# One low part in four by an accumulating transfer in a split-float32 decoder layer

## The chip, the cores and the metric

The kernel runs on one core of one Trainium2 chip. The metric is the device time of one execution in microseconds (us). Beside it stands the span of a profiled execution, from the first to the last instruction that the profiler recorded on that core.

## The reference, cut to what matters

A decoder layer on x of 256 x 2048, float32. Everything hangs on large products with weights that are read once from memory:

```python
proj = jnp.einsum('btd,dc->btc', x, w_in[l])      # 2048 -> 17 thousand columns
(q_lat, c_kv, attn_gate, q_idx, k_idx, w_idx,
 x_rnn, rnn_gate, g_a, g_b) = jnp.split(proj, SPLIT_POINTS, axis=-1)
attn = _sparse_attention(q_lat, c_kv, q_idx, k_idx, w_idx, rel_bias, w_uv[l])
branch_a = jnp.einsum('btc,cd->btd', attn * jax.nn.silu(attn_gate), w_branch_a[l])
h = _rglru(x_rnn, ...)
branch_b = jnp.einsum('btc,cd->btd', h * jax.nn.silu(rnn_gate), w_branch_b[l])
merged = jax.nn.sigmoid(g_a) * branch_a + jax.nn.sigmoid(g_b) * branch_b
sub = jnp.einsum('btd,de->bte', merged, w_out[l])
x = _layernorm(ALPHA * x + sub, ln_g[l], ln_b[l])
```

## The kernel before, in words

Each float32 operand of a product is split in two values of the narrower type that TensorE multiplies (float32r): a high part `hi`, the operand rounded to it, and a low part `lo = operand - hi`. A product is then hi·hi + hi·lo + lo·hi.

**Half tiles.** The weights come as 328 half tiles of 128 x 1024 float32, 512 KB each, numbered in the order in which TensorE uses them. A job is a column tile of 128 columns (two halves: `qi`, `ag`, `q`, `xr`, `rg`) or a chunk of 512 columns (eight halves: `ga`, `ba`, `gb`, `bb`). The order of the jobs is qi, ag, q, ga, ba, xr, gb, rg, bb; the last 32 halves are the output projection, `o`. In a column tile the weights are the stationary operand: the first half runs 8 products with `hi` of 512 columns, then 8 with `lo` of 256; the second half runs `lo` first and `hi` last (L203). In a chunk the activations are stationary, and a half is 12 products of 512 columns in the order hi, lo, hi (L756, L757, L758).

**Rings.** `load_to` (L163) brings a half into one of 4 `raw` buffers by a transfer issued by SyncE. `split_to` (L178) makes `hi` (ScalarE, helper line L96) and `lo` (VectorE, helper line L100, a subtraction of `hi` from `raw`), each from a ring of 5 buffers. Both are called from the main loop: while TensorE works on half n, the program issues the split of half n+4 and the load of half n+8. So the split of half i waits until TensorE has finished half i-5, whose buffers it takes, and it is used four halves later.

**Order of the rest.** Each engine runs its instructions in the order in which the program issues them. All other work (gates, attention heads, the recurrence) is cut into steps that the main loop issues at counted ticks, between the products. GpSimd has little: additions of the bias and the mask (L444), clearing of three columns (`xp`, L657), 16 multiplications for the recurrence (`decay`, L703), and at the start of the second `bb` chunk four transfers of 1 MB for the end of the layer (`gb` and `y`, L784 to L787), then one multiplication of `gb` (L877). The four transfers write into memory that the recurrence used, so they wait for its last scan (L711).

Of the kernel before, what the change touches and what calls it, by code (L numbers as in the profile page):

```python
# [13 lines left out]
AF = mybir.ActivationFunctionType  # L14
OP = mybir.AluOpType
# [57 lines left out]
def layer(ctx, tc, ar, out):  # L73
    nc = tc.nc
# [17 lines left out]
    def f(ap):  # L92
        return ap.bitcast(F32)

    def hi_of(hi, src):
        nc.scalar.activation(hi, src, AF.Copy)  # L96

    def lo_of(lo, src, hi):

        nc.vector.tensor_sub(lo, src, f(hi))  # L100
# [7 lines left out]
    def slot(name, dt=F32R):  # L108
        return big.tile([P, 2 * T], dt, name=name, tag="slot", bufs=16)
# [44 lines left out]
    halves = []  # L154
# [7 lines left out]
    raws, parts = {}, {}  # L162
    st = {"load": 0, "split": 0}  # L163

    def load_to(n):
        while st["load"] < min(n, len(halves)):
            i = st["load"]
            kind, a, s = halves[i]
            raw = wpool.tile([P, 1024], F32, name=f"raw{i}", tag="raw", bufs=4)
            if kind == "wt":  # L170
                src = ar["wt"][a, :, s * 8:(s + 1) * 8, :].rearrange("p k c -> p (k c)")
            else:
                src = ar[kind][a, s].rearrange("p k c -> p (k c)")
            nc.sync.dma_start(raw, src)
            raws[i] = raw
            st["load"] += 1

    def split_to(n):  # L178
        while st["split"] < min(n, len(halves)):
            i = st["split"]  # L180
            load_to(i + 1)
            raw = raws.pop(i)
            if NO + 24 <= i < NO + 28:
                pieces = []
                for e in range(2):
                    hi, lo = slot(f"wh{i}_{e}"), slot(f"wl{i}_{e}")
                    c = raw[:, e * 512:(e + 1) * 512]
                    hi_of(hi, c)
                    lo_of(lo, c, hi)
                    pieces.append((hi, lo))  # L190
                parts[i] = pieces
            else:
                hi = wpool.tile([P, 1024], F32R, name=f"hi{i}", tag="hi", bufs=5)
                lo = wpool.tile([P, 1024], F32R, name=f"lo{i}", tag="lo", bufs=5)
                hi_of(hi, raw)
                lo_of(lo, raw, hi)
                parts[i] = (hi, lo)
            st["split"] += 1

# [20 lines left out]
    with pool("pha", side="right") as pha:  # L220
# [29 lines left out]
        for k in range(KT):  # L250
            if k + 1 < KT:
                sp[k + 1] = split_a(k + 1)
            if k + 4 < KT:
                load_a(k + 4)
            else:
                load_to(st["load"] + 1)
            if 8 <= k < 12:
                nc.sync.dma_start(*smalls[k - 8])
            hi, lo = sp.pop(k)
            fl = (k == 0, k == KT - 1)  # L260
            for t in range(2):
                o = psc[t][:, :A_Q]
                x_hi = xs[:, k, t * P:(t + 1) * P]
                x_lo = xs[:, k, T + t * P:T + (t + 1) * P]
                nc.tensor.matmul(o, x_hi, hi[:, :A_Q], start=fl[0], stop=False)
                nc.tensor.matmul(o, x_hi, lo[:, :A_Q], start=False, stop=False)
                nc.tensor.matmul(o, x_lo, hi[:, :A_Q], start=False, stop=fl[1])
            last = k == KT - 1
            for high in (False, True) if last else (True, False):
                for i in range(4):  # L270
                    w = (hi if high else lo)[:, A_Q + i * P:A_Q + (i + 1) * P]
                    mm(psq[i], w, xs[:, k, :], high, fl[0] and high, last and high)
            if k >= 12:
                split_to(k - 11)
# [486 lines left out]
    for kind, i in jobs:  # L761
# [3 lines left out]
        for qt in range(ticks((kind, i))):  # L765
# [25 lines left out]
            else:  # L791
                high = qt in (0, 3)
                w = parts[t // 2][0 if high else 1]
                for kk in range(8):
                    k = qt // 2 * 8 + kk
# [4 lines left out]
            if qt % 2 == 0:  # L800
                split_to(t // 2 + 5)
                load_to(t // 2 + 9)
# [59 lines left out]
    for ec in range(3):  # L862
        pss = [acc_tile(f"pso{ec}_0"), aux_tile(f"pso{ec}_1")]
        for pc in range(8):
            n = NO + ec * 8 + pc
            for i in range(2):
                for t in range(2):
                    products(pss[t], parts[n], i, 2 * pc + i, xs[:, 2 * pc + i, :], t)
                tick(t0)
                t0 += 1  # L870
                if i == 0:
                    split_to(n + 5 + max(0, n - NO - 15) // 2)
                    load_to(n + 9 + max(0, n - NO - 15) // 2)
            parts.pop(n)
        spawn(t0, out_post(ec, pss))
        if ec == 0:
            nc.gpsimd.tensor_scalar(gb[0], gb[0], -0.5, None, op0=OP.mult)  # L877
# [67 lines left out]
```

## Time and profile before

| what | us |
|---|---|
| median of 2 runs (1031.92 to 1036.3) | 1034.11 |
| the profiled execution's own time | 1032.58 |
| its span | 1030.7 |
| TensorE busy | 1014.5 |
| VectorE busy | 683.2 |
| ScalarE busy | 550.8 |
| GpSimd busy | 83.9 |

The granted clock of TensorE was 0.997 over the span. In the profile PE is TensorE (PEld its weight loads), DVE is VectorE, ACT is ScalarE, POOL is GpSimd, SP is SyncE; q0 is the queue of the transfers that GpSimd issues, q1 that of SyncE's. Matmuls overlap in the pipeline, so a matmul's 0.39 us is not its share of the time: in a chunk one starts every 0.227 us. A row of the timeline gives start, duration, engine, line, operation, output and inputs; what stands in brackets is the idle time before it and what ended it. A row of a group gives the busy time, the mean of one in ns and the idle time before. A row of the transfers gives size and the median time from issue to landing.

### The profile page before, as it was taken

The numbers are of one execution on the slowest core, as the hardware profiler recorded it, in microseconds if no ns is written. First come the engines' busy times: TensorE is split into PE (matmuls) and PEld (weight loads), VectorE is DVE, ScalarE is ACT, GpSimd is POOL, SyncE is SP. The second block draws the span as 40 slices with busy tenths as digits, with TensorE's granted clock in tenths as the row PEclk, the third lists the DMA queues.
The fourth block names the chain that finished last, engine by engine and source line by source line (L and its number), as shares of the span: only waits on it lengthen the run. The fifth ranks groups of instructions, "written<-read, shape, count | busy, mean of one in ns | idle before, by whom it ended". The sixth has DMA issues, their size and how long they took to land.

```text
span 1030.7 us, 14867 instructions
## 1 busy us (share of the span) xinstructions
PE 1014.5 (98%) x5464; PEld 880.0 (85%) x5464; DVE 683.2 (66%) x1150; ACT 550.8 (53%) x909; POOL 83.9 (8%) x117
## 2 busy tenths in 40 slices
PE   9999999999999999999999999999999999999995
PEld 8988888988999988888888888888888887888885
DVE  6678587677777676444555788855567876555666
ACT  6666365655555656444343555578655554444441
POOL 0004211101111100000000000000410002000002
PEclk9999999999999999999999999999999999999998
DMA  9845867756566655666666666556666668666552
GB/s 303 271 144 175 280 192 230 231 174 173 184 181 178 194 165 162 187 200 187 198 190 210 204 190 191 164 183 193 194 187 191 189 220 303 189 187 192 188 160 82
DMA packets 60713, 201.41 MB, mean 195 GB/s; under 512 B 6577, under 2 KB 13361, under 8 KB 60001
## 3 DMA queue, kind: packets, MB, share of 16 engines
q1 hardware_dynamic: 59456, 191.35, 60.2%
q0 software_dynamic: 752, 8.42, 2.1%
q8 instruction: 43, 0.70, 0.3%
q10 hardware_dynamic: 432, 0.70, 0.2%
q14 instruction: 30, 0.24, 0.1%
HBM read 198.31 MB, written 6.32 MB: 199 GB/s over the span
## 4 chain that ended last, share of the span: by engine, by line
PE 93%; DVE 2%; ACT 1%; DMA 1%; issue 1%; POOL 0%; ACTq 0%; DVEq 0%; POOLq 0%
PE ps_q L203 17%; PE ps_rg L203 9%; PE ps_xr L203 9%; PE ps_ag L203 6%; PE ps_ga L756 3%; PE ps_gb L758 3%; PE ps_ga L757 3%; PE ps_ga L758 3%; PE ps_ba L757 3%; PE ps_ba L756 3%; PE ps_gb L756 3%; PE ps_gb L757 3%; PE ps_ba L758 3%; PE psq L203 2%; PE ps_bb L756 2%; PE ps_qi L203 2%
## 5 line engine op out<-in xcount | busy, mean ns | idle before, releaser
L100 DVE TENSOR_TENSOR lo<-raw,hi 128x1024 fp32r<-128x1024 f32 x324 | 402.9, 1244 | 308.8 <-ACT hi L96 304.9
L96 ACT ACTIVATE hi<-raw 128x1024 fp32r<-128x1024 f32 x324 | 341.4, 1054 | 185.4 <-PE ps_ba L758 52.6
L203 PE MATMUL ps_q<-xs,hi 128*128 128x512 f32 x512 | 122.4, 391 | 0.0
L203 PEld LDWEIGHTS ps_q<-xs,hi 128*128 128x128 f32 x512 | 94.1, 188 | 18.3
L203 PE MATMUL ps_q<-xs,lo 128*128 128x256 f32 x512 | 71.2, 283 | 0.0
L203 PEld LDWEIGHTS ps_q<-xs,lo 128*128 128x128 f32 x512 | 66.3, 190 | 1.4
L203 PE MATMUL ps_ag<-xs,hi 128*128 128x512 f32 x256 | 61.5, 391 | 0.0
L203 PE MATMUL ps_rg<-xs,hi 128*128 128x512 f32 x256 | 61.2, 391 | 0.0
L203 PE MATMUL ps_xr<-xs,hi 128*128 128x512 f32 x256 | 61.2, 391 | 0.0
L203 PEld LDWEIGHTS ps_ag<-xs,hi 128*128 128x128 f32 x256 | 47.0, 188 | 9.9 <-issue 0.9
L203 PEld LDWEIGHTS ps_rg<-xs,hi 128*128 128x128 f32 x256 | 47.0, 188 | 9.1
L203 PEld LDWEIGHTS ps_xr<-xs,hi 128*128 128x128 f32 x256 | 47.0, 188 | 9.1
L756 PE MATMUL ps_bb<-hi,ub 128*128 128x512 f32 x128 | 50.4, 394 | 0.0
L756 PE MATMUL ps_ga<-hi,xs 128*128 128x512 f32 x128 | 50.0, 391 | 0.0
L758 PE MATMUL ps_ga<-hi,xs 128*128 128x512 f32 x128 | 49.9, 390 | 0.0
L758 PE MATMUL ps_gb<-hi,xs 128*128 128x512 f32 x128 | 49.9, 390 | 0.0
L758 PE MATMUL ps_bb<-hi,ub 128*128 128x512 f32 x128 | 49.9, 389 | 0.0
L757 PE MATMUL ps_gb<-lo,xs 128*128 128x512 f32 x128 | 49.8, 389 | 0.0
L757 PE MATMUL ps_ga<-lo,xs 128*128 128x512 f32 x128 | 49.8, 389 | 0.0
L757 PE MATMUL ps_bb<-lo,ub 128*128 128x512 f32 x128 | 49.8, 389 | 0.0
L756 PE MATMUL ps_ba<-hi,ua 128*128 128x512 f32 x128 | 49.8, 389 | 0.0
L757 PE MATMUL ps_ba<-lo,ua 128*128 128x512 f32 x128 | 49.8, 389 | 0.0
(274 smaller groups left out, 1888.7 us busy)
## 6 DMA issues: line engine op xcount, KB each, us to landing
raw<-in_wt SPq DMA_DIRECT2D x168, 512.0 KB, 4.2
raw<-in_wga SPq DMA_DIRECT2D x32, 512.0 KB, 3.6
raw<-in_wba SPq DMA_DIRECT2D x32, 512.0 KB, 3.5
raw<-in_wgb SPq DMA_DIRECT2D x32, 512.0 KB, 3.5
raw<-in_wbb SPq DMA_DIRECT2D x32, 512.0 KB, 3.6
raw<-in_wo SPq DMA_DIRECT2D x32, 512.0 KB, 4.1
wr<-in_wA SPq DMA_DIRECT2D x15, 424.0 KB, 4.9
dz<-dv POOLq DMA_DIRECT2D x1, 4096.0 KB, 18.7
```

The lines of the kernel that those rows point to most:

```text
L96: nc.scalar.activation(hi, src, AF.Copy)
L100: nc.vector.tensor_sub(lo, src, f(hi))
L203: nc.tensor.matmul(ps[:, :n], w, rhs[:, :n], start=start, stop=stop)
L756: nc.tensor.matmul(o, mh, hi, start=d == 0, stop=False)
L757: nc.tensor.matmul(o, mh, lo, start=False, stop=False)
L758: nc.tensor.matmul(o, ml, hi, start=False, stop=d == KT - 1)
```

## The change

For every fourth half tile from half 62 on (i % 4 == 2 and i >= 60; 66 of them, since half 322 has its own path) the low part is formed in another way: ScalarE writes the negated high part into `lo`, and GpSimd issues a transfer that reads the same 512 KB of weights from memory once more and adds them onto `lo`. VectorE's subtraction is left out there. By stage these are 11 halves of `q`, 8 each of `ga`, `ba`, `xr`, `gb`, `rg`, `bb`, and 7 of `o`.

```diff
+    def weights(i):
+        kind, a, s = halves[i]
+        if kind == "wt":
+            return ar["wt"][a, :, s * 8:(s + 1) * 8, :].rearrange("p k c -> p (k c)")
+        return ar[kind][a, s].rearrange("p k c -> p (k c)")
+
     def load_to(n):
...
-            nc.sync.dma_start(raw, src)
+            nc.sync.dma_start(raw, weights(i))
...
                 hi_of(hi, raw)
-                lo_of(lo, raw, hi)
+                if i % 4 == 2 and i >= 60:
+                    nc.scalar.activation(lo, hi, AF.Copy, scale=-1.0)
+                    nc.gpsimd.dma_start(lo, weights(i), accum_op=OP.add)
+                else:
+                    lo_of(lo, raw, hi)
                 parts[i] = (hi, lo)
```

In the changed program the negation is L198, the transfer L199, and lines behind it stand 5 higher. What moves is best seen on GpSimd. At the change from the `gb` chunks to the `rg` tiles it held, before, the 16 multiplications in a row; the first and last of them:

```order
L703 TENSOR_TENSOR decay<-decay,ri_6026 128x256
L703 TENSOR_TENSOR decay<-decay,ri_6308 128x256
L703 TENSOR_TENSOR decay<-decay,ri_6095 128x256
...
L703 TENSOR_TENSOR decay<-decay,ri_7033 128x256
L784 DMA gb_8720<-in_lng 128x2048
```

and now (lo_7467, lo_7555 and lo_7646 are the low parts of halves 226, 230 and 234):

```order
L199 DMA lo_7467<-in_wgb 128x1024
L708 TENSOR_TENSOR decay<-decay,ri_6056 128x256
L199 DMA lo_7555<-in_wgb 128x1024
L708 TENSOR_TENSOR decay<-decay,ri_6340 128x256
L708 TENSOR_TENSOR decay<-decay,ri_6125 128x256
...
L708 TENSOR_TENSOR decay<-decay,ri_7070 128x256
L199 DMA lo_7646<-in_wt 128x1024
L199 DMA lo_7737<-in_wt 128x1024
```

One transfer stands between the first and the second multiplication, and the next behind all sixteen.

The second place on GpSimd is the start of the second `bb` chunk. Before, the four transfers followed the last `decay` multiplication with nothing between. Now (lo_8553, lo_8659, lo_8736 and lo_8840 are halves 266, 270, 274 and 278):

```order
L199 DMA lo_8553<-in_wbb 128x1024
L199 DMA lo_8659<-in_wbb 128x1024
L199 DMA lo_8736<-in_wbb 128x1024
L789 DMA gb_8774<-in_lng 128x2048
L790 DMA gb_8775<-in_lnb 128x2048
L792 DMA y_8772<-in_xres 128x2048
L792 DMA y_8773<-in_xres 128x2048
L199 DMA lo_8840<-in_wbb 128x1024
L199 DMA lo_8916<-in_wbb 128x1024
```

The four 1 MB transfers now stand behind the low part of half 274 and ahead of that of half 278.

On ScalarE the negation follows its high part at once; in the `gb` chunks (hi_7373 and lo_7374 belong to half 222):

```order
L96 ACTIVATE hi_7350<-raw_7255 128x1024
L697 ACTIVATE a_7362<-ri_6763 128x256
L693 ACTIVATE decay<-ri_6836,c_91 128x256
L694 ACTIVATE ri_6836<-ri_6836,nc_92 128x256
L96 ACTIVATE hi_7373<-raw_7279 128x1024
L198 ACTIVATE lo_7374<-hi_7373 128x1024
L697 ACTIVATE a_7386<-ri_6836 128x256
```

Only the row with L198 is new there.

More of the change, by code (lines that the diff above doesn't have):

```diff
@@ L167, in load_to @@
             i = st["load"]
-            kind, a, s = halves[i]
             raw = wpool.tile([P, 1024], F32, name=f"raw{i}", tag="raw", bufs=4)
[L170 to L173, printed above, removed]
-            nc.sync.dma_start(raw, src)
+            nc.sync.dma_start(raw, weights(i))
             raws[i] = raw
```

## The prediction

> **What bounds the kernel now.** I read the page first, for busy times, then the table by stretches, the waits of TensorE and the groups, and last the timeline of single halves.
>
> ```profile
> span 1030.7 us, 14867 instructions
> PE 1014.5 (98%) x5464; PEld 880.0 (85%) x5464; DVE 683.2 (66%) x1150; ACT 550.8 (53%) x909; POOL 83.9 (8%) x117
> 0.00:43.00 43.00, 42.03 (x258) 39.04 (x259) 27.23 (x43) 25.25 (x42) 0.68 (x6) 1.00 0.90 296
> 164.00:440.00 276.00, 276.00 (x1626) 245.00 (x1625) 189.40 (x422) 158.26 (x323) 28.11 (x37) 1.00 0.62 188
> 660.00:750.00 90.00, 90.00 (x407) 74.78 (x405) 52.48 (x68) 66.35 (x103) 15.57 (x14) 1.00 0.61 187
> 840.00:927.00 87.00, 84.87 (x387) 70.05 (x385) 54.12 (x55) 40.28 (x48) 7.57 (x5) 1.00 0.69 230
> 1012.00:1031.00 19.00, 7.62 (x64) 7.41 (x62) 14.03 (x26) 2.52 (x5) 5.35 (x4) 0.81 0.30 111
> ```
>
> In each stretch the columns are PE, PEld, DVE, ACT, POOL, granted clock, DMA share, GB/s. From 164 us on TensorE is busy without a gap, but for 2 us behind 840 and the 11 us of the last normalisation, which holds no half tile. It is the bound.
>
> ```profile
> PE psm L601 <- DVE gb L593: 2.1, 1, 2.1
> PE ps_ag L203 <- DVE lo L100: 1.6, 2, 1.4
> L100 DVE TENSOR_TENSOR lo<-raw,hi 128x1024 fp32r<-128x1024 f32 x324 | 402.9, 1244 | 308.8 <-ACT hi L96 304.9
> L96 ACT ACTIVATE hi<-raw 128x1024 fp32r<-128x1024 f32 x324 | 341.4, 1054 | 185.4 <-PE ps_ba L758 52.6
> ```
>
> TensorE waited for a low part for 1.6 us in all, in the `ag` tiles that the change leaves alone. VectorE waits for ScalarE, and ScalarE for TensorE to free a buffer.
>
> **The change part by part.** *Removed:* 66 subtractions of 1244 ns, 82 us of VectorE. Nothing on the path waits for them, so they bring 0. This is why I see no way to be faster by 2% (20.7 us): no wait of that size is there to take away. That 2% is also about what a measurement of this kernel can tell from no change.
>
> *Added on ScalarE:* 66 negations. The nearest row is L96, the same size between the same memories, 1.05 us: 70 us in all, and at the fullest, 660 to 750 us, 8 of them make 66.35 into 74.8 of 90 us. Work behind a negation comes 1 us later; the room below shows that a high part can bear it. Cost 0; without that cover, at most 1 us each.
>
> *The low part's new way* is the term that decides. Room first, from half 222 in a `gb` chunk:
>
> ```profile
> 711.66 1.06 ACT L96 ACTIVATE hi<-raw 128x1024 fp32r<-128x1024 f32 x1 [0.41 <-PE ps_gb L758]
> 712.63 0.40 ACT L692 ACTIVATE a<-ri 128x256 f32<-128x256 f32 x1
> 712.76 1.23 DVE L100 TENSOR_TENSOR lo<-raw,hi 128x1024 fp32r<-128x1024 f32 x1 [1.16 <-ACT hi L96]
> 722.57 0.39 PE L757 MATMUL ps_gb<-lo,xs 128*128 128x512 f32 x1
> 766.72 1.05 ACT L96 ACTIVATE hi<-raw 128x1024 fp32r<-128x1024 f32 x1
> 779.19 0.52 PE L203 MATMUL ps_rg<-xs,lo 128*128 128x256 f32 x3
> ```
>
> The high part starts when TensorE frees the buffer (711.66), the next on ScalarE can start 0.97 later, so the negation ends at 713.69; 0.04 to hand over (712.72 to 712.76); first use at 722.57. Room for the transfer: **8.8 us** in chunks. By the last two rows, in the same way, **10.4 us** in `rg` tiles, where eight products with hi run first; I take that for `q` and `xr` too, an estimate on the low side, since other products lie between their halves.
>
> Now the transfer, from issue on GpSimd to landing. No accumulating one is in the trace; the nearest rows:
>
> ```profile
> gb<-in_lng POOLq DMA_DIRECT2D x1, 1024.0 KB, 7.5
> gb<-in_lnb POOLq DMA_DIRECT2D x1, 1024.0 KB, 10.7
> y<-in_xres POOLq DMA_DIRECT2D x2, 1024.0 KB, 15.6
> dv<-vrel POOLq DMA_DIRECT2D x1, 32.0 KB, 4.3
> raw<-in_wgb SPq DMA_DIRECT2D x32, 512.0 KB, 3.5
> 842.97 0.61 POOL L784 DMA_DIRECT2D gb<-in_lng  x1 [91.42 <-DVE ri L711]
> 843.57 0.53 POOL L785 DMA_DIRECT2D gb<-in_lnb  x1
> ```
>
> 1 MB landed at 842.97 + 7.5 = 850.5, the next at 843.57 + 10.7 = 854.3: one behind the other, 3.8 us per MB. So 512 KB moved once is 7.5 - 1.9 = 5.6 us, the lower bound. An add also reads what lies in `lo`; if the two reads follow each other, it costs as 1 MB: **7.5 us**, which I take, as it is the row with as many bytes read. Three passes (read, read, write apart) make 9.4, four 11.3. These rows hold the contention with SyncE's loads, which ran beside them.
>
> If one low part lands late by d, TensorE stalls d; the next one, four halves on, then has d more room, as its buffer was freed before that stall and its use comes after it. So over many, each loses on the mean half of what is over the room, L being the time to landing: (L - 8.8)/2 for the 39 chunk halves, (L - 10.4)/2 for the 27 others. At 7.5 all are hidden, by 1.3 us.
>
> The Trainium skill (Collectives: The Full Stack, "The bandwidth ceiling: the fold count and why AG ≠ RS ≠ AR") says that an add in a transfer halves the rate because it needs two source reads, not because of the adding; its pair of measured rates, 62 and 32 GB/s, stands for double, the same 7.5. No run here shows one yet.
>
> *Moved: GpSimd's queue.* Two places are not hidden.
>
> ```profile
> 734.43 17.12 POOL L703 TENSOR_TENSOR decay<-decay,ri 128x256 f32<-128x256 f32 x16 [76.55 <-DVE decay L700]
> L703 POOL TENSOR_TENSOR decay<-decay,ri x16: 729/740/1742, 734.4 to 750.8; 128x256 f32<-128x256 f32 x16
> 734.64 1.04 ACT L96 ACTIVATE hi<-raw 128x1024 fp32r<-128x1024 f32 x1
> 735.59 1.04 ACT L698 ACTIVATE decay<-decay 128x1024 f32<-128x1024 f32 x1
> 756.92 0.52 PE L203 MATMUL ps_rg<-xs,lo 128*128 128x256 f32 x3
> ```
>
> The transfer of half 230 now waits between the first two of the 16 multiplications for its negation: 735.59 + 1.04, and 0.55 to issue, 737.2, where the second multiplication began at 734.43 + 0.74 = 735.2. The other 15 come 2.0 later and end at 751.55 + 2.0 = 753.6. Half 234's transfer is queued behind them and lands at 753.6 + 7.5 = 761.1; its first use was at 756.92. Stall **4.2 us**. Their result is read by the scans of `rg`, spread over the 90 us behind, and the delay costs nothing there.
>
> ```profile
> 858.36 1.06 ACT L96 ACTIVATE hi<-raw 128x1024 fp32r<-128x1024 f32 x1 [2.71 <-DMA raw<-in_wbb]
> 880.25 0.39 PE L757 MATMUL ps_bb<-lo,ub 128*128 128x512 f32 x1
> ```
>
> The four transfers of `gb` and `y` now wait behind half 274's. Its high part started at 858.36 after 2.71 us of waiting for a load that the four had slowed; with them gone it starts at 855.65, and its transfer is issued at 857.7 and lands at 865.2. The four add 3.8 each: 880.4. Half 278's comes behind them in the same queue: 884.2, against a use at 880.25. Stall **3.9 us**. `gb` and `y` are used behind 927, late enough.
>
> Elsewhere on GpSimd a bias addition or a clearing stands behind one issue (0.6 us) of a negation that ends 2 us after TensorE frees the buffer, and is used ticks later: 0. SyncE's order is unchanged; `raw` comes free earlier.
>
> *Transfers:*
>
> ```profile
> q1 hardware_dynamic: 59456, 191.35, 60.2%
> q0 software_dynamic: 752, 8.42, 2.1%
> ```
>
> 66 x 0.524 = 34.6 MB more; at 60.2% for 191.35 MB that is 11% once, 22% as two passes: 62% becomes some 84%. A load has the 10.9 us between 711.66 and 722.57 (one turn of the buffers), less a high part of 1.06, and lands in 3.5; even doubled it is hidden.
>
> **Sum**, against the profiled execution's own 1032.6 (1.5 under the median shown, 1.9 over its span): 0 + 0 + 4.2 + 3.9 = **1041 us** (1040.7).
>
> **The rivals.**
>
> *Nothing is late.* At one pass (5.6) half 234 stalls 753.6 + 5.6 - 756.92 = 2.3 and half 278 0.1 (857.7 + 5.6 + 15.2 + 1.9 = 880.4): 1035. For it: contention may be less than beside the four. Against it: the add has to read `lo`.
>
> *The transfer becomes the bound* (the other side). If the add takes three passes, L = 9.4: chunks 39 x 0.3 = 11.7, half 234 6.1, half 278 7.8: 1058. Four, 11.3: 39 x 1.25 = 49, 27 x 0.45 = 12, then 8 and 11.5: 1113. With this working the 2% is passed at L = 9.2, 1.7 us above my price, so this is near. For it: 32 KB alone took 4.3, so the share of each row's round trip is large, and a row that must be read, added and written may not overlap with the next. Against it: the four landed 3.8 apart, so rows of plain transfers do overlap.
>
> *Descriptors are held up by VectorE.* GpSimd's multiplication took 0.73 or 1.74 us, so something beside it adds 1.0; added to the transfer, L = 8.5 makes 5.2 + 5.9, 1044, inside my case. If GpSimd has to let two of VectorE's instructions of 1.24 pass, L = 10.0: 23.4 + 6.7 + 9.0, 1072. It decides from the second one on. Against it: `gb` went out while VectorE worked, and its 7.5 holds that.
>
> The Trainium skill (SBUF — State Buffer, "A bandwidth-pool intuition that's wrong (but worth ruling out)") has this as a trap: a transfer from GpSimd of about 620 ns took about 3100 beside a VectorE copy in a two-port mode. By that 2.5 us more, it would be the 1072 too; the subtraction here has two inputs, and no run here shows such a copy beside a transfer.
>
> *The change does nothing that TensorE sees* because the old low parts were hidden anyway: the same as the first rival without its 2.3: 1032.6.
>
> **How the numbers follow.** My case 0.40; nothing late 0.15 and no effect 0.02, all three within 2%: 0.57. Transfer as the bound 0.33, descriptors 0.09: slower 0.42. Faster 0.01, for what I overlooked. The time is that of my case, 1041. Its own range, with L from 6.5 to 9.0, is 1037 to 1050. The range reaches down to no effect, 1033, and up towards four passes, 1105; above that I leave 0.13, below 0.05.
>
> **What would show it.** The landing time of `lo` in the table of transfers: near 7.5 for my case, 9.2 or more for the bound. The waits of TensorE: two long ones, at the low parts of halves 234 (second `rg` tile) and 278 (second `bb` chunk), and none in `ga` and `ba`; a wait at each fourth half there is the second rival. ScalarE's groups should show 66 negations of 1.05, VectorE 258 subtractions. If GpSimd shows long waits ahead of L199 other than for ScalarE, or negations far from 1.05, my reading of the queues is wrong; a TensorE without new waits and a longer time would refute all of it.

## The result and the profile after

The changed kernel takes 1043.65 us (median of 2 runs, 1043.53 to 1043.78) against 1034.11: a ratio of 1.0102, interval 1.0074 to 1.0130. It is slower by about 1%, and within 2%. The forecast was 1041. Later runs of the kernel before have medians of 1031.6 to 1032.1, and the ratios of the experiments are taken against those; against them the changed kernel is 1.1% slower. The profiled execution took 1043.78 us with a span of 1042.0, so 11.3 us of span are to be found. First the page, with the two groups that the change touches and the two main queues:

```profile
span 1042.0 us, 14981 instructions
PE 1017.8 (98%) x5464; PEld 880.4 (84%) x5464; DVE 615.4 (59%) x1084; ACT 615.7 (59%) x975; POOL 137.1 (13%) x183
q1 hardware_dynamic: 59456, 191.35, 56.8%
q0 software_dynamic: 10256, 43.03, 21.4%
L100 DVE TENSOR_TENSOR lo<-raw,hi 128x1024 fp32r<-128x1024 f32 x258 | 329.7, 1279 | 341.6 <-ACT hi L96 334.3
L198 ACT ACTIVATE lo<-hi 128x1024 fp32r<-128x1024 f32 x66 | 70.0, 1060 | 2.1
```

VectorE lost 66 subtractions, ScalarE took 66 negations of 1.06 us, and GpSimd's queue moved 34.6 MB more. The table of transfers and the waits of TensorE:

```profile
lo<-in_wt POOLq DMA_DIRECT2D x27, 512.0 KB, 7.3
lo<-in_wba POOLq DMA_DIRECT2D x8, 512.0 KB, 7.0
lo<-in_wbb POOLq DMA_DIRECT2D x8, 512.0 KB, 7.4
raw<-in_wgb SPq DMA_DIRECT2D x32, 512.0 KB, 4.5
PE ps_bb L762 <- DMA lo<-in_wbb: 7.2, 1, 7.2
PE ps_gb L762 <- DVE lo L100: 1.9, 1, 1.9
PE ps_rg L208 <- DMA lo<-in_wt: 1.1, 1, 1.1
```

An accumulating transfer lands in 7.0 to 7.4 us (the medians of the stages), and 64 of the 66 landed in time or within 0.2 us of it. There are three new waits, and one of them is for VectorE. The room can be read at half 222 again:

```profile
712.97 1.06 ACT L198 ACTIVATE lo<-hi 128x1024 fp32r<-128x1024 f32 x1
714.33 0.86 POOL L199 DMA_DIRECT2D lo<-in_wgb  x1 [10.02 <-ACT lo L198]
722.79 0.39 PE L762 MATMUL ps_gb<-lo,xs 128*128 128x512 f32 x1
```

The negation ends at 714.03, GpSimd issues 0.30 later, and from there to the use are 8.46 us.

**Where the 11.3 us are.** Comparing when TensorE begins the same half in both profiles gives the shift along the span: 0.2 us from half 28 to 226; 2.8 at half 234; 4.4 from half 246 to 270; 2.0 at 274; 11.1 at 282; 11.4 at 318. Two places therefore hold it, both on GpSimd. At the multiplications for the recurrence 4.2 us are lost. At the second `bb` chunk the shift first falls by 2.4, since the kernel before had a stall there that is gone, and then rises by 9.1.

The first place, the timeline of GpSimd and VectorE:

```profile
737.29 0.87 POOL L199 DMA_DIRECT2D lo<-in_wgb  x1 [1.99 <-ACT lo L198]
737.88 10.68 POOL L708 TENSOR_TENSOR decay<-decay,ri 128x256 f32<-128x256 f32 x15
738.92 10.72 DVE L100 TENSOR_TENSOR lo<-raw,hi 128x1024 fp32r<-128x1024 f32 x1 [0.85 <-ACT hi L96]
748.30 1.08 POOL L199 DMA_DIRECT2D lo<-in_wt  x1
```

The 15 multiplications behind half 230's transfer ran 0.71 us apart, and a subtraction that otherwise takes 1.2 us took 10.72, until they were through. TensorE came to that low part at 747.8 and waited 1.9 us. SyncE's loads, held up behind the subtraction, then went out four in 3 us, and in that crowd half 242's transfer took 10.3 us to land.

The second place, TensorE behind half 278's transfer, and the stretches around it (PEclk, the granted clock, is the third column from the right):

```profile
873.77 0.88 POOL L199 DMA_DIRECT2D lo<-in_wbb  x1 [8.81 <-ACT lo L198]
889.61 0.80 PE L762 MATMUL ps_bb<-lo,ub 128*128 128x512 f32 x1 [7.20 <-DMA lo<-in_wbb]
890.63 0.63 PE L761 MATMUL ps_bb<-hi,ub 128*128 128x512 f32 x1
891.06 0.63 PE L762 MATMUL ps_bb<-lo,ub 128*128 128x512 f32 x1
858.00:882.00 24.00, 24.00 (x111) 19.90 (x110) 11.21 (x12) 11.45 (x13) 3.88 (x6) 1.00 0.98 356
886.20:893.00 6.80, 3.39 (x8) 2.74 (x9) 0.00 (x0) 2.11 (x2) 0.88 (x1) 0.50 0.94 264
```

The transfer engines were 98% busy while the four 1 MB transfers ran; half 278's landed 15.8 us after its issue. After the wait of 7.2 us TensorE ran at half its clock until 893.0: products start 0.43 us apart instead of 0.227, and the 3.4 us cost 1.7 more.

### The profile page after: what moved, and what is told of

Its sections match the earlier page's. It is cut to its first block, busy times and chain, and to the rows that moved or that the text cites. A ratio compares the mean times of both kernels' runs of the same rounds, so it can differ in the third digit from the quotient of the medians.

```text
span 1042.0 us, 14981 instructions
## 1 busy us (share of the span) xinstructions
PE 1017.8 (98%) x5464; PEld 880.4 (84%) x5464; DVE 615.4 (59%) x1084; ACT 615.7 (59%) x975; POOL 137.1 (13%) x183
## 3 DMA queue, kind: packets, MB, share of 16 engines
q1 hardware_dynamic: 59456, 191.35, 56.8%
## 4 chain that ended last, share of the span: by engine, by line
PE 85%; DMA 5%; DVE 4%; issue 3%; ACT 2%; POOL 0%; SPq 0%; DVEq 0%; ACTq 0%; POOLq 0%
PE ps_q L208 17%; PE ps_xr L208 9%; PE ps_rg L208 7%; PE ps_ag L208 3%; PE ps_ga L763 3%; PE ps_ga L761 3%; PE ps_ba L763 3%; PE ps_ba L761 3%; PE ps_ga L762 3%; PE ps_ba L762 3%; PE ps_bb L762 2%; PE ps_bb L763 2%; PE ps_bb L761 2%; PE ps_gb L762 2%; PE ps_gb L763 2%
## 5 line engine op out<-in xcount | busy, mean ns | idle before, releaser
L100 DVE TENSOR_TENSOR lo<-raw,hi 128x1024 fp32r<-128x1024 f32 x258 | 329.7, 1279 | 341.6 <-ACT hi L96 334.3
L198 ACT ACTIVATE lo<-hi 128x1024 fp32r<-128x1024 f32 x66 | 70.0, 1060 | 2.1
L199 POOL DMA_DIRECT2D lo<-in_wt x27 | 23.7, 878 | 209.4 <-ACT lo L198 116.2
```

Source lines behind the costliest of these rows:

```text
L198: nc.scalar.activation(lo, hi, AF.Copy, scale=-1.0)
L199: nc.gpsimd.dma_start(lo, weights(i), accum_op=OP.add)
```

## The experiments

My theory after this profile: the add is hidden, and the whole loss comes from two places in GpSimd's order. The main rival: 66 transfers and their traffic cost a little each, all along.

**Without half 278.** Diff against the changed kernel:

```diff
-                if i % 4 == 2 and i >= 60:
+                if i % 4 == 2 and i >= 60 and i != 278:
```

> Half 278 keeps VectorE's subtraction; the other 65 low parts are formed by the transfer. Theory (the loss is the place in GpSimd's queue behind the four 1 MB transfers): the stall of 7.4 us at half 278 and the 1.75 us behind it at half clock go, so the span falls from 1042.0 to about 1033; as the four then again slow SyncE's loads, up to 2.4 us of the stall that the kernel before had there may come back: 1033 to 1035.5, and no stretch of half clock in 870 to 900 us. Rival (66 transfers cost a little each, 11.3 us over 66 = 0.17 each): 1042 stays, less 0.2.

Measured: 1036.8 us, ratio 1.0038 (1.0022 to 1.0054). TensorE's wait in `bb` and the half clock there are gone, and the old stall at 865 did not come back; one of 66 transfers carried more than half of the loss. The span, 1037.9, was higher than expected: 2.6 us of that lie before the first transfer (a wait at 127 us that varies from run to run), and half 238's transfer, in the crowd behind the multiplications, landed in 11.6 us and cost 2.9.

**Without half 230.**

```diff
-                if i % 4 == 2 and i >= 60:
+                if i % 4 == 2 and i >= 60 and i != 230:
```

> Half 230 keeps VectorE's subtraction. Theory: the transfer between the first and the second of GpSimd's 16 multiplications makes the other 15 run without a break, and they keep VectorE's subtraction of 738.9 us from its memory port for 10.7 us; without it GpSimd and VectorE alternate as before, the longest subtraction in 730 to 760 us is under 2 us, the stall of 2.1 us at 747 us is gone, and with the burst of loads that followed it the landing of 10.3 us at half 242 too (1.25 us): span 1042.0 - 3.4 = 1038.6. Rival (the order of GpSimd's and VectorE's turns is chance): a subtraction of several us there again, 1041 to 1042.

Measured: 1043.82 us, ratio 1.0118 (1.0096 to 1.0140): no gain. The mechanism was as expected, the sum not. GpSimd, VectorE and TensorE there:

```profile
734.32 16.20 POOL L708 TENSOR_TENSOR decay<-decay,ri 128x256 f32<-128x256 f32 x16 [8.49 <-DVE decay L705]
737.59 1.71 DVE L100 TENSOR_TENSOR lo<-raw,hi 128x1024 fp32r<-128x1024 f32 x1 [0.65 <-ACT hi L96]
750.46 0.87 POOL L199 DMA_DIRECT2D lo<-in_wt  x1
760.00 2.29 PE L208 MATMUL ps_rg<-xs,lo 128*128 128x256 f32 x9 [2.94 <-DMA lo<-in_wt]
```

VectorE is free again, but now the multiplications take 16.2 us, since the two engines alternate, and half 234's transfer behind them is issued at 750.46 and is late by 2.9. This is the stall that the prediction had named at half 234; in the changed kernel it was absent only because the multiplications ran undisturbed.

**Without 230 and 278**, and then **without 230, 234 and 278:**

```diff
-                if i % 4 == 2 and i >= 60:
+                if i % 4 == 2 and i >= 60 and i not in (230, 278):
```

> Halves 230 and 278 keep VectorE's subtraction, 64 are formed by the transfer. Theory: both places are gone and all 64 are hidden: the span is that of the kernel before, 1030.7, within 2 us, and the time is not to be told from it. Rival (the traffic itself costs, 34 MB more): about 1041, since 64 of 66 remain.

Measured: 1035.74 us, 1.0037 (1.0022 to 1.0051). Half 234 was late by 3.6 us, as in the run before; nothing else of note. My expectation had overlooked it.

```diff
-                if i % 4 == 2 and i >= 60:
+                if i % 4 == 2 and i >= 60 and i not in (230, 234, 278):
```

> Halves 230, 234 and 278 keep VectorE's subtraction, 63 are formed by the transfer. Theory (two places on GpSimd carry the whole loss: the 16 multiplications, where without half 230 half 234 is late and without half 234 alone the multiplications would still run without a break; and the four 1 MB transfers): none of the 63 is late, and the 2.4 us that the kernel before lost at 865 us, when the four came at 843, stay away as they now come at 862: span 1028 to 1031, ratio 0.997 to 1.000. Rival (the traffic costs too): another late transfer turns up elsewhere and the ratio stays at the 1.0037 of the run without 230 and 278.

Measured: 1031.08 us, 0.9992 (0.9981 to 1.0002), span 1028.3. All of TensorE's waits in this run, and its transfers:

```profile
PE warm L221 <- DVE eps L138: 1.0, 1, 1.0
PE pso L762 <- DMA lo<-in_wo: 0.9, 1, 0.9
PE pss L382 <- DVE rl L393: 0.4, 1, 0.4
PE ps_ag L208 <- DVE lo L100: 0.2, 1, 0.2
q0 software_dynamic: 9824, 41.46, 20.6%
```

63 accumulating transfers and 33 MB of extra traffic cost one wait of 0.9 us. This rules out the main rival. From half 28 to half 272 TensorE kept its distance to the kernel before to within 0.1 us, with 50 transfers in between, and half 274 alone (below), without the other 62, has the same ratio of 0.9992. The kernel is not to be told from the one before. Its span is 2.4 us lower: 1.2 lie before the first transfer, where the wait at 127 us was absent, 2.4 are the old stall at 865 us, and 1.2 were lost again at the late transfer.

**Half 230 alone:**

```diff
-                if i % 4 == 2 and i >= 60:
+                if i == 230:
```

> Half 230 alone is formed by the transfer; all else is as before. Theory (the transfer between the first two multiplications lets the other 15 run without a break and keeps VectorE's subtraction off for 10.7 us): a subtraction of about 10.7 us at 739 us, a stall of TensorE of 2 us at 747 us, loads in a burst behind it: span 1030.7 + 2 to 3 = 1033. Rival (it takes the traffic of the other 65 to make it): no subtraction over 2 us there, span 1030.7.

Measured: 1036.21 us, 1.0038 (1.0021 to 1.0055).

```profile
738.42 0.94 POOL L199 DMA_DIRECT2D lo<-in_wgb  x1 [1.91 <-ACT lo L198]
739.09 10.69 POOL L708 TENSOR_TENSOR decay<-decay,ri 128x256 f32<-128x256 f32 x15
740.05 10.82 DVE L100 TENSOR_TENSOR lo<-raw,hi 128x1024 fp32r<-128x1024 f32 x1 [0.85 <-ACT hi L96]
```

One transfer in the wrong place, without any other traffic, keeps VectorE off for 10.8 us. The run is 0.4% slower. In its profile, whose span is 3.4 us longer, the shift grows by 2.2 us at that place, as expected; 1.4 us stand already at the first half, which the transfer cannot have made.

**Negation only:**

```diff
                     nc.scalar.activation(lo, hi, AF.Copy, scale=-1.0)
-                    nc.gpsimd.dma_start(lo, weights(i), accum_op=OP.add)
```

> The 66 low parts are the negated high parts: the transfers are left out, so the low parts there are other values. It keeps the other two parts of the change, 66 subtractions less on VectorE and 66 negations more on ScalarE. Theory (both cost nothing): span 1030.7 within 1.5 us, no wait of TensorE that the kernel before did not have. Rival (ScalarE's 70 us more delay the work behind them): 3 us or more over it, with new waits of TensorE on ScalarE or VectorE.

Measured: 1032.29 us, 0.9998 (0.9988 to 1.0007), span 1030.2. What was taken from VectorE and given to ScalarE costs and brings nothing.

**A transfer that does not add:**

```diff
-                    nc.gpsimd.dma_start(lo, weights(i), accum_op=OP.add)
+                    nc.gpsimd.dma_start(lo, weights(i))
```

> The 66 transfers do not add: they overwrite lo with the weights, so the low parts are other values (the product is another one). It measures the price of the add alone. Theory (the add costs a second pass of the bytes): landing falls from 7.3 to about 5.6 us and the share of GpSimd's queue from 21.4% to about 11%; half 278 is still late, as it stands behind the four 1 MB transfers, by some 5 to 6 us instead of 7.4: span 1037 to 1041. Rival (the add is free, 7.3 is the price of any such transfer): landing stays at 7.0 to 7.5, share above 18%, span 1042.

Measured: one run of 1039.5 us, span 1037.7.

```profile
lo<-in_wt POOLq DMA_DIRECT2D x27, 512.0 KB, 5.5
lo<-in_wba POOLq DMA_DIRECT2D x8, 512.0 KB, 4.9
q0 software_dynamic: 10256, 43.03, 12.4%
PE ps_bb L762 <- DMA lo<-in_wbb: 3.0, 1, 3.0
```

The add costs some 2 us of landing (4.7 to 5.5 us by stage against 7.0 to 7.4). On the engines: without the 2.1% that the queue had before, 66 transfers hold 10.3% of 1037.7 us when plain and 19.3% of 1042.0 when adding, 1.9 times as much. Half 278 was late by 3.0, less than I expected, as the queue ahead of it was shorter: the last of the four landed 18.8 us after its issue instead of 21.8.

**The four 1 MB transfers from ScalarE's queue:**

```diff
-                nc.gpsimd.dma_start(gb[0], ar["lng"].to_broadcast([P, DM]))
+                nc.scalar.dma_start(gb[0], ar["lng"].to_broadcast([P, DM]))
```

and the other three in the same way.

> All 66 low parts by the transfer, the four 1 MB transfers issued by ScalarE instead of GpSimd. Theory (half 278 is late because it stands behind the four in one queue): in a queue of their own they no longer stand ahead of it; its landing falls from 15.8 to between 7.3 and 11, as they still share the transfer engines; the stall of 7.4 us falls to 0 to 3, the rest (multiplications, 3.7 us) stays: span 1033 to 1037. Rival (the engines are full then, whatever the queue): stall of 5 us or more, 1040 to 1042.

Measured: 1039.71 us, 1.0076 (1.0049 to 1.0103), span 1038.8, of which 2.4 lie before the first transfer; without them it is in the expected range. Halves 274 and 278 landed in 11.3 and 11.9 us, and TensorE waited 3.1 us in two pieces (2.2 for half 274, 0.8 for half 278) instead of 7.2 in one, with no half clock. So the common queue is most of half 278's loss and the crowd on the transfer engines the rest.

**Half 274 alone**, which only puts the four 1 MB transfers later:

```diff
-                if i % 4 == 2 and i >= 60:
+                if i == 274:
```

> Half 274 alone is formed by the transfer, so that the four 1 MB transfers stand behind it and go out at 862 us instead of 843; all else is as before. Theory (the kernel before loses 2.4 us at 865 us because the four slow a load that the first bb chunk's chain stands behind; at 862 no such chain is near): the wait for the transposed products goes, span 1028.3, ratio 0.997 to 0.999. Rival (the gain of 2.4 us in the run without 230, 234 and 278 came from the subtractions taken from VectorE): 1030.7, ratio 1.000.

Measured: 1031.02 us, 0.9992 (0.9983 to 1.0001). The wait for the transposed products at 865 us is gone, and the shift falls by 2.4 us there. But the start of this run was 2.0 us later, and the ratio is just short of what its runs can tell from none. The profile agrees with the theory; the time does not settle it.

**The kernel before, the four spread in the program:**

```diff
-                nc.gpsimd.dma_start(gb[0], ar["lng"].to_broadcast([P, DM]))
-                nc.gpsimd.dma_start(gb[1], ar["lnb"].to_broadcast([P, DM]))
-                for e in range(2):
-                    nc.gpsimd.dma_start(y[e], ar["xres"][e * P:(e + 1) * P, :])
+                late = [(gb[0], ar["lng"].to_broadcast([P, DM])), (gb[1], ar["lnb"].to_broadcast([P, DM]))]
+                late += [(y[e], ar["xres"][e * P:(e + 1) * P, :]) for e in range(2)]
+            if t in (FIN, FIN + 12, FIN + 24, FIN + 36):
+                nc.gpsimd.dma_start(*late[(t - FIN) // 12])
```

> The kernel before, with its four transfers of 1 MB issued 12 ticks apart (at the second bb chunk's ticks 0, 12, and at 8 and 20 of the halves behind) instead of at once; no low part is formed by a transfer. Theory (the four at once slowed a load to 12.6 us and so cost 2.4 us at 865 us): loads in that stretch land in under 8 us, the wait of TensorE for the transposed products at 865 us is gone, span 1028.3, ratio 0.998. Rival (the wait there is VectorE's chain and not the load): ratio 1.000.

Measured: 1032.03 us, 0.9997 (0.9989 to 1.0006). The edit failed its purpose: GpSimd has nothing else to wait for, runs ahead of the ticks and issues all four at once as before (landing 6.4 and 9.6 us, and 14.4 as the median of the last two; three loads of 9 to 11.5 us). It tells nothing of the theory.

**Every second half:**

```diff
-                if i % 4 == 2 and i >= 60:
+                if i % 2 == 0 and i >= 60:
```

> Every second half from 60 on (132) by the transfer. Theory (each costs two passes of its bytes on the 16 engines, 21.4% of 1042 us for 66): the engines would be asked for 57% + 43%, all they have, so transfers queue and land later than 8.5 us: TensorE waits at many halves, span 1075 to 1150 and the transfers' landing 9 to 12 us. Rival (only GpSimd's two places cost): 1042 to 1050, landing 7 to 8.

Measured: one run of 1052.89 us, span 1051.1; my theory was wrong here and the rival nearly right (the span is 1 us over its range).

```profile
lo<-in_wt POOLq DMA_DIRECT2D x54, 512.0 KB, 8.0
lo<-in_wga POOLq DMA_DIRECT2D x16, 512.0 KB, 7.7
q1 hardware_dynamic: 59456, 191.35, 52.2%
q0 software_dynamic: 19760, 77.64, 37.9%
PE ps_bb L762 <- DMA lo<-in_wbb: 11.2, 1, 11.2
PE ps_rg L208 <- DMA lo<-in_wt: 3.4, 1, 3.4
PE ps_gb L762 <- DMA lo<-in_wgb: 2.5, 5, 1.0
```

132 transfers land nearly as fast as 66. I had added shares of engine time as if they were fixed; both queues' shares per byte fell (from 56.8 to 52.2% for the same loads), so 90% are asked for, not 100. The loss is again mostly at the two places (now at half 276 instead of 278), with small waits beginning in `gb`.

**Four buffers instead of five:**

```diff
-                hi = wpool.tile([P, 1024], F32R, name=f"hi{i}", tag="hi", bufs=5)
-                lo = wpool.tile([P, 1024], F32R, name=f"lo{i}", tag="lo", bufs=5)
+                hi = wpool.tile([P, 1024], F32R, name=f"hi{i}", tag="hi", bufs=4)
+                lo = wpool.tile([P, 1024], F32R, name=f"lo{i}", tag="lo", bufs=4)
```

> All 66 by the transfer, with 4 buffers of high and low parts instead of 5, so that a split starts one half (2.72 us) later. Theory (the room is 8.5 us in chunks and falls to 5.8, the landing stays at 7.3, and each stall gives the next its room back, so half of the lack is lost at each): 39 chunk halves x 0.75 = 29 us, in tiles the room falls to about 7.3 and little is lost: span 1042 + 29 = 1071, with waits of TensorE for lo spread over ga, ba, gb, bb and o. Rival (the full lack is lost at each): 39 x 1.5 = 58, 1100. Third (the room is not what decides): 1042.

Measured: one run of 1098.82 us, span 1096.5.

```profile
PE ps_ba L762 <- DMA lo<-in_wba: 9.9, 8, 2.0
PE ps_bb L762 <- DMA lo<-in_wbb: 7.1, 3, 5.9
PE ps_gb L762 <- DMA lo<-in_wgb: 6.3, 4, 2.4
PE pso L762 <- DMA lo<-in_wo: 5.2, 4, 2.0
PE ps_ga L762 <- DMA lo<-in_wga: 3.2, 2, 1.6
```

With 2.72 us less room the waits spread over all chunk stages: 31.7 us, 25.8 without half 278's 5.9, where 29 were expected. So the room decides where TensorE waits. That half of the lack is lost is not shown: the sum of the waits is near that theory, but the chunk transfers landed in 6.1 to 7.1 us and not in 7.3, and the span of 1096.5 is nearer to the rival's 1100 than to 1071. The rest of the 54.5 us over the changed kernel is not the transfers' lateness alone: 5.5 were lost before half 62, and the granted clock fell to half in seven stretches, 27 us in all, behind waits of TensorE. There was no run with four buffers and no transfers, so how the rest splits stays open.

## Why the prediction was right, and where it was not

*TensorE bounds the kernel, and the two edits on VectorE and ScalarE cost 0.* Right: the negation-only run is at 0.9998.

*The landing of 7.5 us, as for 1 MB.* Right: 7.0 to 7.4. The lower bound of 5.6 for one pass was a little high (4.7 to 5.5 measured), and the add weighs as two passes, at 1.9 times the engine time. The Trainium skill (Collectives: The Full Stack, "The bandwidth ceiling: the fold count and why AG ≠ RS ≠ AR") gives the double, for the adding step of a collective; this agrees with it.

*The room of 8.8 us.* Nearly: 8.5. The hand-over from ScalarE to GpSimd takes 0.30 us, and I had used VectorE's 0.04. 1.1 us were left at half 222. In tiles the room was mostly 9.7 to 11.8 us; the 10.4 that was taken from `rg`, and called low for `q`, was high for six of its eleven halves (9.7). The rival in which the transfer is the bound was not far in the room, but one pass more would have been needed, and there was none.

*Half 234, 4.2 us.* The place lost 4.2 us, but in another way, so the step failed and the size was luck. It assumed that the multiplications would go on alternating with VectorE's subtractions. In the changed kernel they did not: half 234's transfer was issued at 748.3, not 753.6, and landed 5.5 us ahead of its use. The loss went to VectorE's subtraction (a wait of 1.9 us) and to the crowd of loads behind it. The stall as I had priced it came in the runs without half 230, at 2.9 and 3.6 us.

*The second `bb` chunk, 3.9 us.* The mechanism was right and the size off: the wait was 7.2 us. Half 274's transfer was issued at 862.0, the expected 857.7 and the 4.4 us by which the span was late there. Half 278's landed at 889.6, 27.6 us behind that issue, where 26.5 were expected (the four took until 885.9 at engines 98% busy). But its use came only 2.0 us later than in the kernel before, as that kernel's stall at 865 us was gone. I had used that old load wait to date the high part, and not followed it to TensorE; it lengthens the wait by 2.4 us and costs nothing net, because the stall went. The terms that were missing from the sum are 1.1 us for the slower transfers and 1.7 us at half clock behind the wait. With the 3.9 forecast they make the 6.7 us net.

*The sum.* 8.1 us forecast, 11.2 measured between the two profiled executions. Of the missing 3.1 us, 2.8 are the half clock and the slower transfers at half 278. The prediction took 2% for about what a measurement can tell from no change; the 1% here was clear of the noise, as the interval of 1.0074 to 1.0130 shows. That everything else is hidden (loads of 4.5 us, GpSimd's other work) held: the run without three halves shows it.

*Descriptors held up by VectorE:* not seen in the changed kernel; all landings but the crowded ones lie at 5.5 to 8.5 us. The contention between the two engines was real, in the other direction: GpSimd's multiplications held up VectorE.

## What to carry to other kernels

When work is handed to a queue that is nearly empty, price the transfer by its bytes (an add counts them about twice) and then walk through the few other things in that queue: here 63 of 66 transfers cost nothing that the time shows, and three in bad places cost the whole 1%. A stall's price has more terms than its length: what it lets run undisturbed elsewhere, the burst of held-back loads, the clock behind it, and the old stalls that it replaces. Placing instructions at later points of the program does not delay them on an engine that waits for nothing.

## What the runs showed of the hardware

**GpSimd can keep VectorE off for a whole row of instructions.** In the kernel before, the multiplications took 0.73 or 1.74 us and the subtractions beside them up to 1.8: each let the other in. Directly behind the transfer of half 230 they started 0.7 us apart, and a two-input subtraction waited for all 15: 10.5 to 10.8 us in six of the seven runs where half 230 was on the transfer path, and 8.7 in the one with every second half, where the last of the row alternated again. In the seven profiles without that transfer none took over 1.8 us beside them. In the changed kernel the multiplications had recorded lengths of 0.9 to 1.05 us there, each beginning before the one ahead had ended. That is not the reason, since behind the transfer that does not add they were 0.71 to 0.75 us long, as in the kernel before, and the subtraction waited all the same:

```profile
738.10 10.47 POOL L708 TENSOR_TENSOR decay<-decay,ri 128x256 f32<-128x256 f32 x15
739.14 10.51 DVE L100 TENSOR_TENSOR lo<-raw,hi 128x1024 fp32r<-128x1024 f32 x1 [0.85 <-ACT hi L96]
```

The Trainium skill (SBUF — State Buffer, "Who interferes with whom") says that VectorE instructions with two inputs in SBUF contend with GpSimd instructions that read it, and that the ports which the two engines share are an exclusive lock. The runs agree, and add that the loser need not get its turn between two instructions. Why it got none behind the transfer stays open.

**Half clock behind waits of TensorE.** After 7.2 us of waiting the granted clock was 0.50 from 886.2 to 893.0; after 2.9 us (without half 230) it was half for 3.4 us; after 1.9 us at 748 us it stayed full. The Trainium skill (TensorE: Matmul & The Clock Gate, 'Part 1: The HAM clock gate (the "warmup" mystery)') gives free-running windows of 3413 ns, at half clock after an idle one; the stretches of 3.4 and 6.8 us agree with one and two of them. But a wait of only 1.8 us at 127 us was followed by such a stretch in three of these runs, so an idle gap shorter than the window can be enough; and the wait of 2.9 us for half 238 in the run without half 278 was followed by none. The first two rows are from the run with half 274 alone, the other two from the run without half 278:

```profile
125.97:129.38 3.41, 1.56 (x13) 1.32 (x12) 2.64 (x9) 2.01 (x3) 0.65 (x1) 1.00 0.46 137
129.40:132.80 3.40, 3.40 (x10) 2.63 (x9) 2.50 (x5) 2.10 (x4) 0.74 (x1) 0.50 0.82 224
774.85:778.27 3.42, 1.76 (x14) 1.77 (x15) 1.67 (x4) 1.97 (x4) 0.86 (x1) 1.00 0.97 274
778.27:781.68 3.41, 3.41 (x18) 2.88 (x17) 1.67 (x3) 1.11 (x2) 0.00 (x0) 1.00 0.97 193
```

Within a run the clock switched only at whole multiples of 3.413 us from its first switch. Cut into such windows, the 14 profiles show that at full clock every window in which TensorE was idle for 2.0 us or more was followed by half clock, and none with 1.7 us or less; in between both happened. The wait at 127 us lay in one window (3.41 - 1.56 = 1.85 us idle); the one of 2.9 us fell into two, with 1.2 and 1.6 us.
